# Eight weight buffers instead of six, paid for with slots and work tiles, in a hybrid decoder trunk

## The chip, the core and the metric

The program runs on one core of a Trainium2 chip. The core has five engines that run side by side, each through its own list of instructions in order: TensorE (PE in the profile, its weight loads are PEld), VectorE (DVE), ScalarE (ACT), GpSimd (POOL) and SyncE (SP), which here only issues DMAs. The metric is the device time of one execution in microseconds (us); of several runs the median counts. Both kernels run one program once, with all weights in HBM at the start.

## The reference

The reference is a decoder trunk of two layers on 256 rows of width 1024, all in fp32. Each layer is

```python
h = h + 0.5 * swiglu(rmsnorm(h, ffn1_norm[i]), ffn1_w_gate[i], ffn1_w_up[i], ffn1_w_down[i])
h = h + mixer(rmsnorm(h, mix_norm[i]))        # layer 0: differential attention, layer 1: Mamba-2 SSD
h = h + memory_cross_attention(rmsnorm(h, xa_norm[i]), mem, ...)
h = h + 0.5 * swiglu(rmsnorm(h, ffn2_norm[i]), ffn2_w_gate[i], ffn2_w_up[i], ffn2_w_down[i])

def swiglu(h, w_gate, w_up, w_down):
    return (jax.nn.silu(h @ w_gate) * (h @ w_up)) @ w_down
```

with a last norm behind layer 1. The hidden width of each of the four feed-forward parts (called FFN 1 to 4 below, in order of time) is 2816, so each reads three matrices of 1024 x 2816 numbers. Differential attention subtracts a second softmax, weighted with a scalar lambda made of four small vectors: exp(sum lq1 lk1) - exp(sum lq2 lk2) + 0.2.

## The kernel before

**Weights.** A weight matrix is read in pieces of 1 MB: a tile of 128 x 2048 fp32 numbers out of the pool `wp`, which has 6 buffers. Each piece is worked off in two *grans* of 128 x 1024 (`Gran.split`, lines 207 to 226). For each gran ACT writes `whi`, the piece rounded to fp32r (L224), and DVE writes `wlo`, the rest (L225). TensorE then multiplies three times (`mm3`, L262 to L264): high by high, high by low, low by high. `whi` and `wlo` have 4 buffers each (`hp`), and the grans are split two ahead of the one that TensorE works on (`AHEAD`). A weight buffer comes free when the second gran's `wlo` has been written; only then may SP issue the load that takes its place. SP's queue is in order.

**The sets.** The gate and up projections of an FFN are cut into blocks of 512 columns, c = 0 to 4, and a half block, c = 5. Two of them (in FFN 2 to 4: c = 0 and c = 5) are done plainly. The blocks c = 1 to 4 (in FFN 1: 2 to 4) are each one *set*, made by `seven` in the manner of Strassen: seven products of half the size in each direction instead of eight. With the four weight pieces b11 and b21 (up, first and second half of the rows) and b12 and b22 (gate), the seven right-hand sides are, in the order in which a set uses them: x1 = b11 + b12, then b11, x2 = x1 + b22, b22, x3 = b12 + b22, b21, x4 = x2 + b21. The sums x1 and x2 are DVE additions of a whole piece (L203; x1 takes a buffer of its own, x2 is written over it). x3 and x4 are accumulating DMAs: GpSimd issues two of 512 KB (L199) that read the weight once more and add it onto the buffer, as soon as its earlier content has been split. So a set of 512 columns loads four pieces and two again. Each right-hand side is two grans of six matmuls on TensorE.

**The hosts.** A set has more work for DVE per matmul than a plain product. So `share` mixes other grans, the *hosts*, between the seven products: `counts` gives, for each of the seven positions, how many hosts come before that product. A host is a gran with 12 matmuls. In FFN 2 to 4 the 22 hosts are, in this order, four grans of up of c = 0, four of the half block, and fourteen of the down projection of the hidden blocks that are done (`d0`, `d1`). What the counts don't use comes behind the last set.

**The order.** The kernel is written as a list of units. Every stage calls `pipe.pe(us)` after its matmuls, which advances a written clock; `pipe.after(us, f)` puts a piece of evacuation work f at a due time on that clock. The result is a program order. For the first two units the order of PE, DVE, ACT and SP is kept as written, for the SSD mixer that of PE; for all other units the framework's scheduler orders each engine's instructions by its own estimate of when they can run, with program order as the priority. Each engine's list is fixed when the program is built.

**Other pools.** `slot` hands out 128 x 512 tiles (2 KB on each partition) of the pool `sp`, 32 of them, for everything that lives some time: hidden activations, q, k, v, SSD states. `work` hands out tiles for passing results: up to 256 columns from tag "v" with 9 buffers (1 KB each), else from tag "w" with 10 (2 KB each).

**Lambda.** `lam_col` runs as an extra in the third set of FFN 1. DVE multiplies and sums (L717, L718), ACT takes the exponential (L719), then DVE subtracts (L720) and subtracts 0.2 (L721). The value is read by the softmax of the differential attention (`probs`, L982 on).

Of the kernel before, what the change touches and what calls it, by code (L numbers as in the profile page):

```python
# [12 lines left out]
ALU = mybir.AluOpType  # L13
AX = mybir.AxisListType

P = 128
# [41 lines left out]
def trunk(ctx, tc, a, out):  # L58
    nc = tc.nc


    const = ctx.enter_context(tc.tile_pool(name="const", bufs=1))
    wp = ctx.enter_context(tc.tile_pool(name="wp", bufs=6))
    hp = ctx.enter_context(tc.tile_pool(name="hp", bufs=4))
    xp = ctx.enter_context(tc.tile_pool(name="xp", bufs=8))
    sp = ctx.enter_context(tc.tile_pool(name="sp", bufs=32))
    wk = ctx.enter_context(tc.tile_pool(name="wk", bufs=10))
    sm = ctx.enter_context(tc.tile_pool(name="sm", bufs=3))
    pacc = ctx.enter_context(tc.tile_pool(name="pacc", bufs=8, space=bass.MemoryType.PSUM))
    dram = ctx.enter_context(tc.tile_pool(name="dram", bufs=1, space=bass.MemoryType.DRAM))  # L70
# [9 lines left out]

    def work(name, n=512, dt=F32):

        return wk.tile([P, n], dt, name=name, tag="v", bufs=9) if n <= 256 else wk.tile([P, n], dt, name=name, tag="w")


    ident = const.tile([P, P], F32, name="ident")
# [53 lines left out]
    pipe = Pipe()  # L140
# [171 lines left out]
    def wide(parts, norm, name, fin, eng=None, single=False):  # L312


        ws = [[W(src, k, 4, c0, n) for k in range(0, KT, 4)] for src, c0, n in parts]

        def run(*gr):
            ps = [acc(name) for _ in range(2)]
            for g in use(gr):
                for k in range(g.nk):  # L320
                    kt = g.k0 + k
                    xh, xl = pipe.need(norm.x, kt)
                    if single and kt < 4:

                        for i, (l, r) in enumerate(((xh, g.hi), (xl, g.hi), (xh, g.lo))):
                            for t in range(2):
                                nc.tensor.matmul(ps[t], lhsT=l[:, t * P:(t + 1) * P], rhs=r[:, k, :],
                                                 start=kt == 0 and i == 0, stop=False)
                        pipe.pe(1.36)
                        continue  # L330
                    for t in range(2):
                        ts = slice(t * P, (t + 1) * P)
                        mm3(ps[t], xh[:, ts], xl[:, ts], g.hi[:, k, :], g.lo[:, k, :], kt == 0, kt == KT - 1)
                        pipe.pe(0.68)
            fin(ps)
        cut = [(k, 1) for k in range(KT)] if single else ((0, 2), (2, 2), (4, 2), (6, 2))
        units.append(([Gran(k, nk, *((w[k // 4], 0, n) for w, (_, _, n) in zip(ws, parts)),
                            eng=eng if k in ((3, 5) if single else (6,)) else None) for k, nk in cut], run))

    def stream(parts, norm, name, fin):  # L340

        ws = [Pair(parts, k) for k in range(0, KT, 4)]
        ps = []

        def step(g):
            if not ps:
                ps.extend(acc(name) for _ in range(2))
            for k in range(g.nk):
                kt = g.k0 + k
                xh, xl = pipe.need(norm.x, kt)  # L350
                for t in range(2):
                    ts = slice(t * P, (t + 1) * P)
                    mm3(ps[t], xh[:, ts], xl[:, ts], g.hi[:, k, :], g.lo[:, k, :], kt == 0, kt == KT - 1)
                    pipe.pe(0.68)
            if kt == KT - 1:
                fin(ps)
        return [(Gran(k, 2, (ws[k // 4], 0, 512)), step) for k in (0, 2, 4, 6)]
# [111 lines left out]
    def combine(y, out, waits, pre=()):  # L469

        raw = {}

        def part(t, h):
            return [v2(y[2 * h + p])[:, :, t * P:(t + 1) * P] for p in range(2)]

        def mix(i, l, r, op):
            raw[i] = work("sraw")
            o, l, r = ([v2(x[:, p * S:(p + 1) * S]) for p in range(2)] if not isinstance(x, list) else x
                       for x in (raw[i], raw[l] if isinstance(l, int) else l, r))
            for p in range(2):  # L480
                nc.vector.tensor_tensor(o[p], l[p], r[p], op=op)

        def cut(i):
            hi, lo = slot("s_hi", F32R), slot("s_lo", F32R)
            nc.scalar.copy(hi, raw[i])
            nc.vector.tensor_tensor(lo, raw[i], hi.bitcast(F32), op=ALU.subtract)
            out[i] = (hi, lo)
        steps = [*pre, lambda: mix(0, part(1, 0), part(1, 1), ALU.subtract), lambda: cut(0),
                 lambda: mix(2, 0, part(0, 0), ALU.subtract), lambda: mix(1, 2, part(0, 1), ALU.add), lambda: cut(1),
                 lambda: cut(2), lambda: mix(3, part(0, 0), part(1, 0), ALU.subtract), lambda: cut(3)]  # L490
        for f, w in zip(steps, waits):
            pipe.after(w, f)

    class Norm:
# [15 lines left out]
        def square(self, c):  # L510
            for t in range(2):
                junk = work("sq")
                nc.scalar.activation(junk, h[t][c], AF.Square, accum_out=self.ss[:, 2 * c + t:2 * c + t + 1])
            self.n += 1
            if self.n == 2:
                s = sm.tile([P, 16], F32, name="nsum", tag="nsum")
                nc.vector.tensor_tensor(s[:, 0:2], self.ss[:, 0:2], self.ss[:, 2:4], op=ALU.add)
                self.col = rpow(s[:, 0:2], 1.0 / D, 2, "rcol")
                if self.first:
                    pipe.after(1.5, self.scaled)  # L520
# [134 lines left out]
    lam = const.tile([P, 4], F32, name="lam")  # L655
# [58 lines left out]
    def lam_col():  # L714
        pr = work("lampr", 128).rearrange("p (c d) -> p c d", c=2)
        l4 = lqk.rearrange("p (c t) d -> p c t d", t=2)
        tc.keep_in_program_order(nc.vector.tensor_tensor(pr, l4[:, :, 0, :], l4[:, :, 1, :], op=ALU.mult))  # L717
        nc.vector.tensor_reduce(lam[:, 0:2], pr, axis=AX.X, op=ALU.add)  # L718
        nc.scalar.activation(lam[:, 0:2], lam[:, 0:2], AF.Exp)  # L719
        nc.vector.tensor_tensor(lam[:, 2:3], lam[:, 1:2], lam[:, 0:1], op=ALU.subtract)  # L720
        nc.vector.tensor_scalar(lam[:, 3:4], lam[:, 2:3], 0.2, None, op0=ALU.subtract)  # L721

    nlam = lam[:, 3:4]

# [50 lines left out]
    def ffn_hidden(nm, l, norm, fin, extra=None):  # L775
# [11 lines left out]
        def gate_fin(c):  # L787
            def fin(ps):
                if c == 0:
                    pipe.after(T["gate"], gated(c, ps, 512))  # L790
                else:
                    gated(c, ps, 512)()
            return fin

        def up_fin(c, o=0, n=512):
            def fin(ps):
                if o:
                    gated(c, ps, n)()
                us = box.pop(c)
                for t in range(2):  # L800
                    nc.vector.scalar_tensor_tensor(us[t][:, :n], ps[t][:, o:o + n], norm.col[:, t:t + 1], us[t][:, :n],
                                                   op0=ALU.mult, op1=ALU.mult)
                pipe.after(T["hid"], lambda: turn(c, us, n))
                extras(c)
            return fin
# [53 lines left out]
        wide([(wg, 0, 512)], norm, "gate", gate_fin(0), **({} if units else dict(single=True, eng=nc.gpsimd)))  # L859
        c = HID // 512  # L860
        half = stream([(wg, c * 512, 256), (wu, c * 512, 256)], norm, "gateup", up_fin(c, 256, 256))
        six, eight, ten = [1, 1, 1, 0, 1, 1, 1], [2, 1, 1, 1, 1, 1, 1], [2, 1, 2, 1, 2, 1, 1]
        if norm is first_norm:
            wide([(wu, 0, 512)], norm, "up", up_fin(0))
            n = half + stream([(wg, 512, 512)], norm, "gate", gate_fin(1)) + stream([(wu, 512, 512)], norm, "up", up_fin(1))
            counts = {2: eight, 3: eight, 4: ten}
        else:
            n = stream([(wu, 0, 512)], norm, "up", up_fin(0)) + half
            counts = {1: six, 2: six, 3: six, 4: [1, 0, 1, 0, 1, 0, 1]}
        wd = a[nm + "_w_down"][l]  # L870

        def part(half, ps):
# [9 lines left out]
        for c, k in counts.items():  # L882
            s = seven((wu, c * 512), (wg, c * 512), norm.x, norm.s, seven_fin(c), (0, 1, 3, 2, 5, 4, 6), "dve")
            steps += share(n[:sum(k)], s, k)
            n = n[sum(k):]
# [4 lines left out]
    def ffn(nm, l, norm, nxt, extra=None):  # L890
        fin = upd(0.5, nxt)
        hid, wd = ffn_hidden(nm, l, norm, fin, extra)
        weave(down(wd, 1, [(12, 4), (16, 4)], hid, [], 12, fin))
# [630 lines left out]
    def last(norm):  # L1524
# [48 lines left out]
        def first_half(half, banks):  # L1573
            for t in range(2):
                for q in range(2):
                    evac(banks[t][:, q * 256:(q + 1) * 256], t, q)
        hid, wd = ffn_hidden("ffn2", 1, norm, first_half, {12: final_gain})
        banks = {}

# [91 lines left out]
```

## Time and profile before

| | |
|---|---|
| median of 3 runs | 1277.52 us (1272.74, 1277.52, 1277.61) |
| profiled execution, its own time | 1276.76 us |
| its span, first to last instruction | 1274.9 us |
| mean granted TensorE clock | 0.998 |
| busy share of the span | PE 98%, PEld 84%, DVE 83%, ACT 69%, POOL 13% |
| read from HBM | 267.52 MB |

Outside the span lie 1276.76 - 1274.9 = 1.9 us. A matmul is counted busy from its start to a modelled end, and neighbours overlap; so PE's idle time shows only pauses, and what a pause costs is read from the distance of two starts. Idle time of DVE, ACT and the DMA queues costs nothing in itself; it matters where TensorE waits behind it.

### The profile page before, as it was taken

How to read it: one execution, taken by the hardware profiler on the slowest of the kernel's cores; microseconds unless marked ns; L12 is line 12 of the kernel's file. 1: busy time of each engine (PE TensorE's matmuls, PEld its weight loads, DVE VectorE, ACT ScalarE, POOL GpSimd, SP SyncE). 2: the span in 40 equal slices, each digit the busy share in tenths (PEclk: the TensorE clock that was granted, in tenths of full speed). 3: DMA queues.
4: the chain of work that ended last, by engine and by line, in shares of the span. 5: the costliest groups of instructions: out<-in, count | busy, mean ns of one | idle time of the engine just before them, and what ended most of it. 6: DMA issues, size and time to landing. Idle time of an engine off the chain costs nothing.

```text
span 1274.9 us, 18150 instructions
## 1 busy us (share of the span) xinstructions
PE 1254.1 (98%) x6751; PEld 1070.9 (84%) x6751; DVE 1057.5 (83%) x1451; ACT 877.6 (69%) x1394; POOL 161.4 (13%) x139
## 2 busy tenths in 40 slices
PE   9999999999999999999999999999999999999997
PEld 7778888788988887888887889999998898888786
DVE  6989776886877898888888976798998987998796
ACT  6766765686666876677776766677776775877673
POOL 1111002200100010100101100022222100101110
PEclk9999999999999999999999999999999999999999
DMA  9877965344685688995798986665544685698891
GB/s 334 220 224 237 321 231 168 131 138 161 144 272 150 194 247 248 251 319 157 231 248 237 261 279 193 207 199 166 184 147 165 153 244 166 169 260 220 275 279 36
DMA packets 158315, 269.79 MB, mean 212 GB/s; under 512 B 6889, under 2 KB 43410, under 8 KB 158226
## 3 DMA queue, kind: packets, MB, share of 16 engines
q1 hardware_dynamic: 137744, 229.75, 53.0%
q0 software_dynamic: 19744, 38.28, 17.5%
q8 instruction: 53, 0.87, 0.3%
q10 hardware_dynamic: 738, 0.59, 0.1%
q14 instruction: 36, 0.29, 0.1%
HBM read 267.52 MB, written 1.08 MB: 211 GB/s over the span
## 4 chain that ended last, share of the span: by engine, by line
PE 78%; DVE 9%; DMA 8%; issue 3%; ACT 2%; POOL 0%; POOLq 0%; DVEq 0%; ACTq 0%; SPq 0%
PE out L263 7%; PE out L264 7%; PE out L262 7%; DMA w<-in_ffn_w_gate_dram 7%; PE seven L263 6%; PE seven L264 6%; PE seven L262 6%; DVE wlo L225 4%; PE xs L264 2%; PE xs L262 1%; PE xs L263 1%; DVE w L203 1%; PE mk L262 1%; PE mk L264 1%; PE mk L263 1%
## 5 line engine op out<-in xcount | busy, mean ns | idle before, releaser
L225 DVE TENSOR_TENSOR wlo<-w,whi 128x1024 fp32r<-128x1024 f32 (+2 forms) x532 | 641.4, 1220 | 128.0 <-ACT whi L224 119.5
L224 ACT CAST whi<-w 128x1024 fp32r<-128x1024 f32 (+2 forms) x534 | 551.8, 1040 | 272.8 <-PE out L264 98.3
L262 PE MATMUL out<-whi,hid_hi 128*128 128x512 f32 x336 | 132.5, 394 | 0.0
L263 PE MATMUL out<-wlo,hid_hi 128*128 128x512 f32 x336 | 131.3, 391 | 0.7 <-DVE wlo L225 0.6
L264 PE MATMUL out<-whi,hid_lo 128*128 128x512 f32 x336 | 131.4, 391 | 0.0
L262 PE MATMUL seven<-whi,s_hi 128*128 128x512 f32 x272 | 106.8, 393 | 0.0
L263 PE MATMUL seven<-wlo,s_hi 128*128 128x512 f32 x272 | 106.1, 390 | 0.4 <-DVE wlo L225 0.4
L264 PE MATMUL seven<-whi,s_lo 128*128 128x512 f32 x272 | 106.0, 390 | 0.0
L203 DVE TENSOR_TENSOR w<-w 128x2048 f32<-128x2048 f32 x32 | 73.2, 2288 | 25.7 <-DMA w<-in_ffn_w_gate_dram 24.6
L199 POOL DMA_DIRECT2D w<-in_ffn_w_gate_dram x30 | 36.9, 1467 | 346.3 <-DVE w L203 189.9
L263 PE MATMUL seven<-wlo,xh 128*128 128x512 f32 x180 | 71.0, 394 | 7.5 <-DVE wlo L225 7.4
L263 PEld LDWEIGHTS out<-wlo,hid_hi 128*128 128x128 f32 x336 | 63.2, 188 | 14.9 <-DVE wlo L225 2.3
L264 PEld LDWEIGHTS out<-whi,hid_lo 128*128 128x128 f32 x336 | 63.1, 188 | 14.0 <-DVE hid_lo L855 1.0
L262 PEld LDWEIGHTS out<-whi,hid_hi 128*128 128x128 f32 x336 | 63.1, 188 | 12.4
L262 PE MATMUL seven<-whi,xh 128*128 128x512 f32 x180 | 70.1, 390 | 0.0
L264 PE MATMUL seven<-whi,xl 128*128 128x512 f32 x180 | 70.1, 390 | 0.0
L199 POOL DMA_DIRECT2D w<-in_ffn_w_up_dram x30 | 36.6, 1251 | 233.7 <-DVE wlo L225 221.2
L263 PEld LDWEIGHTS seven<-wlo,s_hi 128*128 128x128 f32 x272 | 51.1, 188 | 10.8 <-DVE wlo L225 0.8
L264 PEld LDWEIGHTS seven<-whi,s_lo 128*128 128x128 f32 x272 | 51.1, 188 | 10.7
L262 PEld LDWEIGHTS seven<-whi,s_hi 128*128 128x128 f32 x272 | 51.1, 188 | 10.0
L263 PEld LDWEIGHTS seven<-wlo,xh 128*128 128x128 f32 x180 | 33.8, 188 | 17.7 <-DVE wlo L225 10.9
L262 PEld LDWEIGHTS seven<-whi,xh 128*128 128x128 f32 x180 | 33.9, 188 | 7.2
(397 smaller groups left out, 3020.9 us busy)
## 6 DMA issues: line engine op xcount, KB each, us to landing
w<-in_ffn_w_up_dram SPq DMA_DIRECT2D x40, 1024.0 KB, 6.8
w<-in_ffn_w_down_dram SPq DMA_DIRECT2D x40, 1024.0 KB, 8.4
w<-in_ffn_w_gate_dram SPq DMA_DIRECT2D x38, 1024.0 KB, 7.9
w<-in_ssd_w_in_dram SPq DMA_DIRECT2D x24, 1024.0 KB, 5.4
w<-in_xa_w_kv_dram SPq DMA_DIRECT2D x16, 1024.0 KB, 5.1
w<-in_ffn_w_gate_dram POOLq DMA_DIRECT2D x30, 512.0 KB, 8.5
w<-in_ffn_w_up_dram POOLq DMA_DIRECT2D x30, 512.0 KB, 7.4
w<-in_da_w_in_dram SPq DMA_DIRECT2D x12, 1024.0 KB, 5.2
```

The lines of the kernel that those rows point to most:

```text
L199: nc.gpsimd.dma_start(self.t[:, k:k + 2, :], w.src[r0:r0 + 2 * P, w.c0:w.c0 + w.n] .rearrange("(k p) c -> p k c", p=P), accum_op=ALU.add)
L203: nc.vector.tensor_tensor(self.t, self.l.t, w.t, op=ALU.add)
L224: nc.scalar.copy(hv, src)
L225: self.eng.tensor_tensor(self.lo[:, :, o:o + n], src, hv.bitcast(F32), op=ALU.subtract)
L262: nc.tensor.matmul(o, lhsT=lh, rhs=rh, start=start, stop=False, skip_group_check=onto)
L263: nc.tensor.matmul(o, lhsT=lh, rhs=rl, start=False, stop=False, skip_group_check=onto)
L264: nc.tensor.matmul(o, lhsT=ll, rhs=rh, start=False, stop=stop, skip_group_check=onto)
```

## The change

The pool `wp` gets 8 buffers instead of 6 (16 KB more on each partition). `sp` falls from 32 to 28 slots (8 KB less), the "w" work tiles from 10 to 7 (6 KB less), the "v" tiles from 9 to 6 (3 KB less). The last two steps of lambda are put at a due time 6.0 us later on the written clock. In FFN 2 to 4 the hosts of the four sets change from 6, 6, 6, 4 to 6, 5, 6, 5: the second set loses the host before its second product (b11), the last set gains one before its sixth product (b21). The order of the 22 hosts stays.

```diff
-    wp = ctx.enter_context(tc.tile_pool(name="wp", bufs=6))
+    wp = ctx.enter_context(tc.tile_pool(name="wp", bufs=8))
...
-    sp = ctx.enter_context(tc.tile_pool(name="sp", bufs=32))
-    wk = ctx.enter_context(tc.tile_pool(name="wk", bufs=10))
+    sp = ctx.enter_context(tc.tile_pool(name="sp", bufs=28))
+    wk = ctx.enter_context(tc.tile_pool(name="wk", bufs=7))
...
-        return wk.tile([P, n], dt, name=name, tag="v", bufs=9) if n <= 256 else wk.tile([P, n], dt, name=name, tag="w")
+        return wk.tile([P, n], dt, name=name, tag="v", bufs=6) if n <= 256 else wk.tile([P, n], dt, name=name, tag="w")
...
         nc.scalar.activation(lam[:, 0:2], lam[:, 0:2], AF.Exp)
-        nc.vector.tensor_tensor(lam[:, 2:3], lam[:, 1:2], lam[:, 0:1], op=ALU.subtract)
-        nc.vector.tensor_scalar(lam[:, 3:4], lam[:, 2:3], 0.2, None, op0=ALU.subtract)
+
+        def minus():
+            nc.vector.tensor_tensor(lam[:, 2:3], lam[:, 1:2], lam[:, 0:1], op=ALU.subtract)
+            nc.vector.tensor_scalar(lam[:, 3:4], lam[:, 2:3], 0.2, None, op0=ALU.subtract)
+        pipe.after(6.0, minus)
...
-        six, eight, ten = [1, 1, 1, 0, 1, 1, 1], [2, 1, 1, 1, 1, 1, 1], [2, 1, 2, 1, 2, 1, 1]
+        five, six = [1, 0, 1, 0, 1, 1, 1], [1, 1, 1, 0, 1, 1, 1]
+        eight, ten = [2, 1, 1, 1, 1, 1, 1], [2, 1, 2, 1, 2, 1, 1]
...
-            counts = {1: six, 2: six, 3: six, 4: [1, 0, 1, 0, 1, 0, 1]}
+            counts = {1: six, 2: five, 3: six, 4: five}
```

## The prediction

> **What bounds the kernel now.** The page first: TensorE is busy for all but 20.8 of 1274.9 us, so the change can win only pauses of TensorE. Next who it waited for, longest in total first:
>
> ```profile
> span 1274.9 us, 18150 instructions
> PE 1254.1 (98%) x6751; PEld 1070.9 (84%) x6751; DVE 1057.5 (83%) x1451; ACT 877.6 (69%) x1394; POOL 161.4 (13%) x139
> ...
> PE seven L263 <- DVE wlo L225: 7.8, 8, 1.9
> PE up L263 <- DVE lam L721: 1.9, 1, 1.9
> ...
> PE xs L264 <- DVE xq_lo L1052: 1.2, 1, 1.2
> PE xs L262 <- ACT xq_hi L1051: 0.7, 1, 0.7
> PE out L263 <- DVE wlo L225: 0.6, 2, 0.3
> ```
>
> The reader sees a dozen short waits, nearly all for DVE's `wlo`. Who held DVE up stands in the waits of DVE, and whom the loads wait for in those of SP's queue:
>
> ```profile
> DVE w L203 <- DMA w<-in_ffn_w_gate_dram: 24.6, 11, 4.5
> SPq L161 <- DVE wlo L225: 791.6, 161, 14.9
> ```
>
> DVE stood 24.6 us before the sums x1 and x2 (L203) until a gate piece had landed; every `wlo` queued behind such a sum stood with it. SP stood 791.6 us until a `wlo` gave a buffer free. So the loop is: buffer free, load, sum, `wlo`, matmul. The chain of waits shows the load in it each time (start, us):
>
> ```profile
> 74.48 9.36 DMA w<-in_ffn_w_gate_dram
> 341.72 12.34 DMA w<-in_xa_w_q_dram
> ...
> 673.57 9.53 DMA w<-in_ffn_w_gate_dram
> ```
>
> One turn of it, in the third set of FFN 4, from the timeline of SP, DVE and PE:
>
> ```profile
> 1163.39 1.22 DVE L225 TENSOR_TENSOR wlo<-w,whi 128x1024 fp32r<-128x1024 f32 x1
> 1166.38 0.37 SPq L161 DMA_DIRECT2D w<-in_ffn_w_down_dram  x1
> 1171.88 0.37 SPq L161 DMA_DIRECT2D w<-in_ffn_w_gate_dram  x1
> 1176.50 1.21 DVE L225 TENSOR_TENSOR wlo<-w,whi 128x1024 fp32r<-128x1024 f32 x1
> 1182.23 2.29 DVE L203 TENSOR_TENSOR w<-w 128x2048 f32<-128x2048 f32 x1 [4.51 <-DMA w<-in_ffn_w_gate_dram]
> 1184.44 1.22 DVE L225 TENSOR_TENSOR wlo<-w,whi 128x1024 fp32r<-128x1024 f32 x1
> 1185.71 0.50 PE L263 MATMUL seven<-wlo,xh 128*128 128x512 f32 x1 [1.90 <-DVE wlo L225]
> 1188.05 0.50 PE L263 MATMUL seven<-wlo,xh 128*128 128x512 f32 x1 [0.67 <-DVE wlo L225]
> ```
>
> SP issues b22 at 1171.88, the moment a buffer comes free; it lands some 10.3 us later, DVE had been free since 1177.71, and TensorE pays 1.90 + 0.67 us.
>
> **The change, part by part.**
>
> *Two more weight buffers.* With eight, each load may start at the buffer release two places earlier in the row. For the b22 above the releases were, going back, 1171.88, 1166.38 (the down load went out on it) and the end of the `wlo` at 1164.61 (1163.39 + 1.22). Issued there, with the same 10.3 us, it lands at about 1174.9, 2.8 us before DVE gets to x2. The 4.51 us go, and both pauses with them. What is late next is the `wlo` queue itself: the second product's `wlo` would be done 4.5 us earlier for a pause of 1.9, so about 2.6 us of slack is left there. The same count for the other loads of the chain moves each of them forward by more than its wait. I take all of these pauses as gone. Two pauses stay, in the first set of FFN 1:
>
> ```profile
> 37.76 0.50 PE L263 MATMUL seven<-wlo,s_hi 128*128 128x512 f32 x1 [0.40 <-DVE wlo L225]
> 47.51 0.50 PE L263 MATMUL seven<-wlo,xh 128*128 128x512 f32 x1 [1.91 <-DVE wlo L225]
> ```
>
> DVE is busy without a break there (it builds the first mixed inputs), and no DMA is late. So of the 7.8 us, 7.8 - 0.40 - 1.91 = 5.5 go, and the 0.6 of `out`. The 1.2 + 0.7 of `xs` in the first cross attention go as well: there ACT's in-order queue stood for a piece of the q weights, with the `xq_hi` that TensorE wanted behind it:
>
> ```profile
> 354.15 1.05 ACT L224 CAST whi<-w 128x1024 fp32r<-128x1024 f32 x1 [2.01 <-DMA w<-in_xa_w_q_dram]
> ```
>
> *The pause called `lam`.* The waits put 1.9 us down to L721, but DVE's rows show the x2 sum before it, held by b22 (issued at 74.48):
>
> ```profile
> 83.93 2.29 DVE L203 TENSOR_TENSOR w<-w 128x2048 f32<-128x2048 f32 x1 [3.27 <-DMA w<-in_ffn_w_gate_dram]
> 86.14 0.15 DVE L720 TENSOR_TENSOR lam<-lam 128x1 f32<-128x1 f32 x1
> 87.34 0.14 DVE L721 TENSOR_SCALAR lam<-lam 128x1 f32<-128x1 f32 x1
> 84.97 0.39 PE L264 MATMUL seven<-whi,s_lo 128*128 128x512 f32 x1
> 85.19 0.39 PE L262 MATMUL up<-whi,xh 128*128 128x512 f32 x1
> 87.48 0.50 PE L263 MATMUL up<-wlo,xh 128*128 128x512 f32 x1 [1.90 <-DVE lam L721]
> 88.00:91.60 3.60, 3.60 (x10) 2.78 (x10) 3.60 (x5) 0.00 (x0) 0.00 (x0) 0.53 0.00 0
> ```
>
> The last row is a stretch (length, busy time and count on PE, PEld, DVE, ACT and POOL, granted clock, DMA share, GB/s). After the pause the clock falls to 0.53: 10 matmuls in 3.60 us, where 16 would start at a distance of 0.22 to 0.23 (84.97 to 85.19). Six missing are 1.4 us. So this place costs 1.9 + 1.4 = 3.3 us, and the earlier load takes it away. Moving L720 and L721 issues the same two instructions later, no DMA, past no queue but DVE's own; it takes 0.15 + 0.14 us out of a stretch that DVE then gets through anyway, and puts them into a later one. I take 0 for it, bounded by 0.3 either way. Without the move DVE, no longer held by x2, could have come to L720 before ACT's exponential was done; the later due time covers that.
>
> The Trainium skill, "TensorE: Matmul & The Clock Gate", section "Part 1: The HAM clock gate (the "warmup" mystery)", says the clock is halved after at least one idle window of about 3.4 us. By that rule a pause of 1.9 us costs itself alone, and the gain of this place would be 1.9 instead of 3.3; the row with 0.53 speaks against it here.
>
> *A pause costs more than the idle time shown.* 85.19 to 87.48 is 2.29 us between two starts that else lie 0.23 apart: 2.06 lost for 1.90 idle. 0.16 more on each of the eleven pauses that go (6 seven, 2 out, 1 up, 2 xs): 1.8 us.
>
> *Slots and work tiles.* These cost where fewer buffers than live tiles are left. I counted, from first write to last read of each tile in the timeline. Of the 405 slot tiles at most 26 live at once (the 26th is written in the first row); of the 181 "w" tiles at most 5; of the 81 "v" tiles at most 6, for under 0.1 us:
>
> ```profile
> 339.87 0.68 DVE L1052 TENSOR_TENSOR xq_lo<-xq,xq_hi 128x512 fp32r<-128x512 f32 x1
> 280.16 0.69 DVE L1025 TENSOR_TENSOR on<-po,orc 128x512 f32<-128x512 f32 x1 [1.12 <-POOL orc L466]
> 960.08 0.40 ACT L1470 ACTIVATE junk<-y 128x256 f32<-128x256 f32 x1
> ```
>
> 28, 7 and 6 are enough. If the buffers go round in order of release, the tightest reuse lies 6.3 us after the release for slots, 8.3 for "w" and 2.2 for "v". Cost 0. Without that cover a waiting `junk` or `yo` would stand at the head of ACT's or DVE's queue with the `whi` and `wlo` behind it; the shortest reach is in the SSD part, eight groups, and I bound it by 0 to 0.4 us (one `junk`) for each.
>
> *The hosts.* The last set has the front x1, b11, host, x2 after the change as before; its new host comes behind x3, before b21, and gives 12 x 0.23 = 2.7 us of matmuls before x4 is wanted. Before, x4 was late there:
>
> ```profile
> 1239.55 1.05 ACT L224 CAST whi<-w 128x1024 fp32r<-128x1024 f32 x1 [1.24 <-DMA w<-in_ffn_w_up_dram]
> 533.27 0.50 PE L263 MATMUL seven<-wlo,xh 128*128 128x512 f32 x1 [0.43 <-DVE wlo L225]
> 1207.40 2.29 DVE L203 TENSOR_TENSOR w<-w 128x2048 f32<-128x2048 f32 x1 [1.56 <-DMA w<-in_ffn_w_gate_dram]
> ```
>
> That wait didn't reach TensorE, so the host gains cover and no time. The second set takes over the short front: TensorE comes to b11 and x2 2.7 us earlier, DVE only one `wlo` (1.2 us) earlier. The nearest rows are the last set's, which had that front: up to 0.7 us of pauses in a set (the 0.43 above and one `out` of the waits, 0.6 / 2), and that with x1 held up by its load (1.56 us above). In the second set x1 waited 1 us or less. So 0 to 0.7 for each of three sets; I take 0.3: 0.9 us.
>
> **Sum**, against the profiled execution (1276.76 us, 0.76 under the median of the runs): 5.5 + 0.6 + 1.9 + 3.3 + 1.8 = 13.1 gained, 0.9 lost: 1264.6, against the median 1265.3. I say **1265 us**. Bounds: everything gone, the first set's 2.3 us too, gives about 1261; slots and hosts at their worst (8 x 0.4 + 3 x 0.7 = 5.3 in place of 0.9) about 1270.
>
> **The rivals.**
>
> *DVE stays behind* (chance 0.20). Each engine's list is ordered anew by the scheduler's estimate; if x1 and x2 are put earlier because their loads come earlier, DVE may meet another late piece, and the `wlo` behind it wait as before. For: DVE is 83% busy on the whole. Against: 24.6 us of its waits are for these loads alone. About half of the gain stays: 1271 (1268 to 1274).
>
> *The buffers bring no earlier load* (0.12): the change doesn't do what it says. SP's queue is in order, so a load that is due early can stand behind one that still waits. For: the rows tell only that the load in front waited for its buffer, not what the one behind it would do. Against: the releases two places back were there each time. Then 1276 to 1278.
>
> *Slower: x4's accumulating DMAs come too late* (0.10). Two more megabytes may be under way when they are issued.
>
> ```profile
> 1190.62 2.44 POOL L199 DMA_DIRECT2D w<-in_ffn_w_up_dram  x2 [17.99 <-DVE wlo L225]
> 1205.92 1.05 ACT L224 CAST whi<-w 128x1024 fp32r<-128x1024 f32 x1 [0.45 <-PE out L264]
> w<-in_ffn_w_up_dram POOLq DMA_DIRECT2D x30, 512.0 KB, 7.4
> w<-in_xa_w_kv_dram SPq DMA_DIRECT2D x16, 1024.0 KB, 5.1
> ```
>
> In the third set of FFN 4 they are issued from 1190.62 on, and the `whi` of x4 starts at 1205.92, 15.3 us later. 1.2 + 7.4 us leaves about 6.7; behind two more loads of 5.1 us it would be 3.5 too late, which the split's lead of two grans covers only in part. Over 15 sets it decides from 0.9 us a set (13.1 / 15); at 1.5 it gives 22.5 - 13.1 = +9.4: 1287. Against: the loads start earlier and so end earlier, and their number is the same; ACT waited for x4 only 1.24 us even in the last set.
>
> The Trainium skill, "DMA: Bandwidth & Descriptors", section "Queues, rings and completion order", says that each DMA engine takes turns between the queues that have work, packet by packet. By that rule more loads waiting on SP's queue take no larger share from GpSimd's than one does, and this rival falls away; no row here shows the turns.
>
> **How the numbers follow.** Forecast 0.58, with 1260 to 1269; the rivals 0.20, 0.12 and 0.10. The range of 8 in 10 takes in the forecast, the first rival and most of the second: 1260 to 1277. A measurement of this kernel tells about 0.5% from no change, 6.4 us. Faster by more (under 1271.1): all of the forecast and half of the first rival, 0.67; within 0.5%: the rest of that one, the second and a part of the third, 0.25; slower 0.08.
>
> **What would show it.** Right: in DVE's waits, L203 for the gate pieces falls from 24.6 to under 5 us; PE's waits for `wlo` in `seven` from 7.8 to about 2.5, all in FFN 1; no stretch with the clock at 0.5 near 88 us; no `xs` wait in the first cross attention; ACT's wait for x4 gone. Wrong: DVE still standing at L203; new waits for slots, named by `slot` or `work` tiles; `whi` of x4 waiting for in_ffn_w_up; pauses at b11 or x2 of the second set above 0.7 us.

## The result, and the profile after

| | before | after |
|---|---|---|
| median | 1274.70 us (1272.55 to 1278.11, 7 runs) | 1269.06 us (1267.77 to 1270.46, 7 runs) |
| ratio, 95% interval | | 0.9948 [0.9932, 0.9965] |
| the same two kernels on a second chip | 1271.78 us (29 runs) | 1270.74 us (12 runs), 0.999 [0.9976, 1.0005] |
| profiled execution: own time, span | 1276.76, 1274.9 us | 1269.06, 1267.2 us |

The kernel became faster by 5.6 us in the first measurement. In the second the medians differ by 1.0 us, and the interval takes in no change at all. Neither is the 12.2 us forecast. One of the 29 runs, of 1778.78 us at a mean clock of 0.655, was a slow one and is not in the ratios. The profiled executions differ by 7.7 us of span. The page of the kernel after:

```profile
span 1267.2 us, 18142 instructions
...
PE 1251.8 (99%) x6751; PEld 1070.5 (84%) x6751; DVE 1057.7 (83%) x1451; ACT 878.6 (69%) x1394; POOL 161.6 (13%) x139
```

TensorE is idle for 15.4 us now, 5.4 less than before. Whom it waited for (total, times, longest):

```profile
PE seven L263 <- DVE wlo L225: 2.2, 2, 1.9
PE seven L262 <- DVE p L830: 1.8, 3, 0.9
...
PE gate L327 <- ACT whi L224: 1.0, 1, 1.0
PE gate L263 <- DVE wlo L225: 1.0, 2, 0.8
PE out L264 <- DVE hid_lo L858: 0.9, 1, 0.9
```

Of the pauses that the prediction quoted only the two in the first set of FFN 1 are left, but three names are new: `p`, `gate` (in FFN 1, at 7, 14 and 68 us) and `hid_lo`. What held DVE up and what held SP up:

```profile
DVE w L203 <- DMA w<-in_ffn_w_gate_dram: 6.2, 6, 2.3
```

```profile
SPq L161 <- DVE wlo L225: 781.5, 159, 15.1
```

DVE's wait before the sums fell from 24.6 to 6.2 us. SP waits for buffers about as long as before (791.6): it doesn't wait less, it waits for releases that lie earlier. The turn of the loop that the prediction followed, b22 of the third set of FFN 4, now looks like this (SP, then DVE):

```profile
1155.10 0.37 SPq L161 DMA_DIRECT2D w<-in_ffn_w_gate_dram  x1
```

```profile
1169.01 1.21 DVE L225 TENSOR_TENSOR wlo<-w,whi 128x1024 fp32r<-128x1024 f32 x1
1170.15 2.28 DVE L203 TENSOR_TENSOR w<-w 128x2048 f32<-128x2048 f32 x1
1172.35 1.22 DVE L225 TENSOR_TENSOR wlo<-w,whi 128x1024 fp32r<-128x1024 f32 x1
```

The load goes out 15.1 us before its sum, and the row of the sum has no bracket any more: DVE doesn't stand there.

Where the 7.7 us of span came from, from the first matmul of one part to that of the next in the traces (us; the kernel with the pools alone, `e1_pools`, is the first experiment):

| | before | after | pools alone |
|---|---|---|---|
| to the first product of FFN 1's first set | 37.0 | 37.7 | 37.8 |
| rest of FFN 1 | 158.31 | 157.05 | 156.80 |
| differential attention | 136.49 | 136.48 | 136.48 |
| first cross attention | 80.98 | 78.47 | 78.49 |
| FFN 2 | 178.56 | 177.93 | 175.60 |
| FFN 3 | 190.79 | 189.50 | 188.59 |
| SSD mixer | 227.78 | 227.65 | 227.66 |
| second cross attention | 79.63 | 79.61 | 79.61 |
| FFN 4 | 178.96 | 176.37 | 175.20 |
| from the last matmul's end to the end of the span | 6.42 | 6.41 | 6.43 |

The last two columns hold the main finding. Between these executions the pools alone took 12.2 us off the span; the rest of the change gave 4.5 of them back, nearly all in FFN 2 to 4 (2.33, 0.91 and 1.17). These are single executions. That of the kernel before lies 2 to 5 us above its medians, so the medians put the gain of the pools lower, at 7.7 to 8.3 us (below). A second execution with the pools alone (`e15_pools_again`) took 0.8 us more in FFN 2 and 1.0 more in FFN 3, so the 0.91 of FFN 3 says nothing; FFN 4 differs by 0.02.

### The profile page after: what moved, and what is told of

It is laid out like the page before. It is cut to its first block, busy times and chain, and to the rows that moved or that the text cites. A ratio compares the mean times of both kernels' runs of the same rounds, so it can differ in the third digit from the quotient of the medians.

```text
span 1267.2 us, 18142 instructions
## 1 busy us (share of the span) xinstructions
PE 1251.8 (99%) x6751; PEld 1070.5 (84%) x6751; DVE 1057.7 (83%) x1451; ACT 878.6 (69%) x1394; POOL 161.6 (13%) x139
## 4 chain that ended last, share of the span: by engine, by line
PE 87%; DVE 7%; issue 2%; DMA 2%; ACT 2%; POOL 0%; POOLq 0%; DVEq 0%; ACTq 0%
PE out L264 9%; PE out L263 8%; PE out L262 8%; PE seven L262 8%; PE seven L263 7%; PE seven L264 7%; DVE wlo L225 3%; PE xs L264 2%; DMA w<-in_ffn_w_gate_dram 2%; PE xs L262 2%; PE xs L263 2%; PE mk L262 1%; PE xq L263 1%; PE mk L264 1%; PE xq L264 1%
## 5 line engine op out<-in xcount | busy, mean ns | idle before, releaser
L203 DVE TENSOR_TENSOR w<-w 128x2048 f32<-128x2048 f32 x32 | 73.2, 2286 | 6.3 <-DMA w<-in_ffn_w_gate_dram 6.2
L264 PEld LDWEIGHTS seven<-whi,xl 128*128 128x128 f32 x180 | 33.9, 189 | 7.1
```

The source lines that it names most:

```text
L203: nc.vector.tensor_tensor(self.t, self.l.t, w.t, op=ALU.add)
L264: nc.tensor.matmul(o, lhsT=ll, rhs=rh, start=False, stop=stop, skip_group_check=onto)
```

## The experiments

Twelve kernels in three groups of four, each group on one chip beside fresh runs of the kernel before: its medians there were 1272.75 (23 runs), 1271.78 (29 runs) and 1272.74 us (14 runs). The theory at the start: the buffers carry the gain, the hosts and lambda move little. The rivals: the scheduler's new order of DVE's list takes a part back; or the hosts do.

### The parts by themselves

`e1_pools`: only the four buffer numbers of the change.

```diff
-            counts = {1: six, 2: five, 3: six, 4: five}
+            counts = {1: six, 2: six, 3: six, 4: [1, 0, 1, 0, 1, 0, 1]}
...
-        pipe.after(6.0, minus)
+        minus()
```

(the diff is against the kernel after). Expected:

> The kernel before with the pools of the change alone (wp 8, sp 28, wk 7 and 6), lambda and the hosts as before. Theory A (the earlier loads bring the whole gain, the new hosts of the second set cost 2.3 us: three pauses of 0.46 + 0.88 + 0.46 us idle before x3, for DVE's subtraction p at the line of c12, with 0.16 more on each): ratio to before 0.994 (7.9 us faster), no PE wait of seven for p, the pauses of the sets 3 and 4 in FFN 2 to 4 gone. Theory B (the hosts carry a part of the gain, the pools less): ratio 0.997 or above, pauses in the last sets left.

Measured: 1264.48 us (1263.64 to 1266.62, 6 runs), ratio 0.9937 [0.9925, 0.995]. TensorE's waits:

```profile
PE gate L263 <- DVE wlo L225: 2.6, 1, 2.6
PE seven L263 <- DVE wlo L225: 2.1, 2, 1.9
```

Apart from the start two pauses in FFN 1 are left; no `p`, no `hid_lo`, and in FFN 2 to 4 one pause of 0.2 us (three, the longest 0.5, in `e15_pools_again`). So the pools are the whole gain, 8.3 us on this chip, and more than the change brings there (`e7_lam_undone` below: 2.8). DVE's wait is another matter:

```profile
DVE w L203 <- DMA w<-in_ffn_w_gate_dram: 14.6, 10, 3.2
```

The faster kernel has more than twice the 6.2 us of the kernel after, and 16.6 in `e15_pools_again`. This sum doesn't tell how late TensorE is: it counts where TensorE runs out of `wlo` behind it, and in FFN 2 to 4 it hardly does here.

`e2_hosts_undone`: the kernel after with the old hosts, that is pools and lambda.

```diff
-            counts = {1: six, 2: five, 3: six, 4: five}
+            counts = {1: six, 2: six, 3: six, 4: [1, 0, 1, 0, 1, 0, 1]}
```

> The changed kernel with the hosts of before (6, 6, 6, 4). Theory A: 2 us faster than the changed kernel, ratio 0.994 to 0.993, no PE wait of seven for p; the last sets stay without pauses, since x1 is no longer late there. Theory B: slower than the changed kernel, ratio 0.996 or above, with pauses for wlo back in the last sets.

Measured: 1265.72 us (1263.99 to 1271.03), 0.995 [0.9932, 0.9968]; no wait for `p`. Its profiled execution was a long one (span 1269.2), with a pause of 1.5 us in FFN 3 behind an early sum. Within the intervals it is the same as the pools alone.

`e3_hosts_alone`: the kernel before with the new hosts.

```diff
-            counts = {1: six, 2: six, 3: six, 4: [1, 0, 1, 0, 1, 0, 1]}
+            counts = {1: six, 2: [1, 0, 1, 0, 1, 1, 1], 3: six, 4: [1, 0, 1, 0, 1, 1, 1]}
```

> The kernel before with the new hosts alone. Theory A: 2 us slower than before, ratio 1.001 to 1.002: the second set pauses for p, and the pauses of the last set (0.43, 0.35 and 0.27 idle) stay, because its front is the same. Theory B: faster than before, ratio 0.998 or less.

Measured: 1277.36 us (1273.55 to 1285.91, 12 runs), 1.0045 [1.0028, 1.0063]: 4.6 us slower than before, where 2 were expected. No wait for `p` here; with six buffers the pauses come elsewhere, three for a `wlo` of the down projection in the last sets (TensorE's waits):

```profile
PE out L263 <- DVE wlo L225: 5.1, 3, 2.2
PE seven L263 <- DVE wlo L225: 4.5, 6, 1.9
```

The longest, in FFN 4 (timeline, DVE, then PE): DVE stands 1.81 us at a `hid_lo` for ACT's `hid_hi`, and the `wlo` that TensorE wants is behind it.

```profile
1220.04 1.29 DVE L855 TENSOR_TENSOR hid_lo<-htp,hid_hi 128x512 fp32r<-128x512 f32 x2 [1.81 <-ACT hid_hi L854]
1221.24 2.35 DVE L225 TENSOR_TENSOR wlo<-w,whi 128x1024 fp32r<-128x1024 f32 x2
```

```profile
1222.51 0.80 PE L263 MATMUL out<-wlo,hid_hi 128*128 128x512 f32 x1 [2.25 <-DVE wlo L225]
```

`e7_lam_undone`: the kernel after with lambda's end at its old place.

```diff
-        pipe.after(6.0, minus)
+        minus()
```

> The changed kernel with the end of lambda at its old place. Theory A: no difference to the changed kernel within 0.3 us, ratio 0.9948. Rival: with x2 no longer late, DVE comes to the first subtraction before ACT's exponential is done, waits for it 1 us or more and holds the wlo behind it: a PE pause near 80 us, 1 to 2 us slower than the changed kernel, ratio 0.996.

Measured: 1269.95 us (1268.14 to 1273.91, 12 runs), 0.9978 [0.9963, 0.9993]. It has the same waits as the kernel after: `p` 1.4 us in three, `hid_lo` 1.0, and none for `lam`. Against `e1_pools` on the same chip it differs by the hosts alone: 1269.95 - 1264.48 = 5.5 us. Lambda's move shows no effect that the runs can tell, here or in `e2_hosts_undone` (1.2 us above `e1_pools`, inside the intervals).

### Which order of DVE costs

The kernel after showed DVE's x1 sums (L203) far ahead in its list. In FFN 2 the x1 sum of the third set (timeline, DVE, then PE):

```profile
473.50 2.28 DVE L203 TENSOR_TENSOR w<-w 128x2048 f32<-128x2048 f32 x1
475.70 0.68 DVE L858 TENSOR_TENSOR hid_lo<-htp,hid_hi 128x512 fp32r<-128x512 f32 x1
476.31 2.35 DVE L225 TENSOR_TENSOR wlo<-w,whi 128x1024 fp32r<-128x1024 f32 x2
478.57 0.68 DVE L830 TENSOR_TENSOR p<-p,seven 128x512 f32<-128x512 f32 x1
```

```profile
479.31 0.50 PE L262 MATMUL seven<-whi,s_hi 128*128 128x512 f32 x1 [0.46 <-DVE p L830]
```

The sum stands 22 us ahead of its product (495.3) and in front of the `p` of the second set, whose PSUM bank the x3 product needs. With the pools alone `p` comes first:

```profile
479.17 0.68 DVE L827 TENSOR_TENSOR p<-p,seven 128x512 f32<-128x512 f32 x1
...
481.88 2.29 DVE L203 TENSOR_TENSOR w<-w 128x2048 f32<-128x2048 f32 x1 [0.79 <-DMA w<-in_ffn_w_gate_dram]
```

At the end of FFN 2 of the kernel after the same happens with the first sum of FFN 3, ahead of both `hid_lo`, and there its load isn't even landed:

```profile
568.88 2.29 DVE L203 TENSOR_TENSOR w<-w 128x2048 f32<-128x2048 f32 x1 [0.83 <-DMA w<-in_ffn_w_gate_dram]
571.08 0.68 DVE L858 TENSOR_TENSOR hid_lo<-htp,hid_hi 128x512 fp32r<-128x512 f32 x1
```

```profile
571.82 0.73 PE L264 MATMUL out<-whi,hid_lo 128*128 128x512 f32 x2 [0.88 <-DVE hid_lo L858]
```

`e5_after_again`: the kernel after, unchanged, as the mark of the second chip.

> The changed kernel once more, as the mark for the three others and for what differs from one execution to the next. Expected 0.995 to before, pauses at the same places as in the first profile, but the 3.4 us at half clock, which stood behind the pause at 48 us in the first profile and behind the one at 85 us in the kernel before, at another place or missing: whether a pause is followed by it is chance, so it is no term of any edit.

Measured: 1270.74 us (1268.13 to 1275.43, 12 runs), 0.999 [0.9976, 1.0005], not the 0.995 expected. The same list, another execution (DVE, then PE):

```profile
573.11 2.29 DVE L203 TENSOR_TENSOR w<-w 128x2048 f32<-128x2048 f32 x1 [2.53 <-DMA w<-in_ffn_w_gate_dram]
```

```profile
576.05 0.50 PE L264 MATMUL out<-whi,hid_lo 128*128 128x512 f32 x1 [2.59 <-DVE hid_lo L858]
```

The place that cost 0.88 us before costs 2.59 here, because the load lands 1.7 us later, counted from the FFN's first matmul. A sum put ahead of a load that hasn't landed makes the time hang on that load. At 68 us, in FFN 1, the pause is 2.58 in place of 0.81.

`e8_front_kept`: the kernel after, the second set gives up the host before b21 and keeps the one before b11.

```diff
-            counts = {1: six, 2: five, 3: six, 4: five}
+            counts = {1: six, 2: [1, 1, 1, 0, 1, 0, 1], 3: six, 4: five}
```

> The changed kernel, with the second set's host taken away before b21 (1, 1, 1, 0, 1, 0, 1) and its front left as before. Theory L (the lost host in the front makes DVE late): the three pauses of seven for p go, 2.3 us faster than the changed kernel. Theory S (the scheduler puts the DVE sum x1 of the next set earlier, ahead of what TensorE wants, since its loads come earlier): the pauses for p may go or move, but pauses behind early sums stay, gain under 1.5 us.

Measured: 1270.06 us (1268.02 to 1273.58), 0.9987 [0.9977, 0.9997]. The three `p` waits are gone and nothing is won. The wait for `hid_lo` stays (3.25 us in its profile), and in FFN 4, which has no pause of 0.3 us or more, the kernel needs 176.36 us against 175.20 with the pools alone: seven distances between starts of 0.33 to 0.45 us instead of 0.23, in four places, 69 to 107 us after the FFN's first matmul. So what the hosts cost is not the `p` waits alone: the seven distances add up to 1.0 of the 1.16 us.

`e10_sums_in_order`: the kernel after, the sums kept in program order on DVE.

```diff
-                nc.vector.tensor_tensor(self.t, self.l.t, w.t, op=ALU.add)
+                tc.keep_in_program_order(nc.vector.tensor_tensor(self.t, self.l.t, w.t, op=ALU.add))
```

> The changed kernel, with each DVE sum x1 and x2 held at its place in program order, so that the scheduler can't move it forward; the loads stay early. Theory S: the pause for gate near 68 us, those for p in the second sets and that for hid_lo near 571 us go, 3 to 5 us faster than the changed kernel (ratio to before 0.991 to 0.9925), and DVE's waits for gate pieces at the sums fall from 6.2 us to under 3. Theory L: the sums now come just before the wlo that need them, the second set's short front still has DVE late, pauses at b11 or x2 of that set; no faster than the changed kernel.

Measured: 1270.13 us (1269.38 to 1273.6, 12 runs), 0.9984 [0.997, 0.9997]. DVE has no wait left for a gate piece, and `p`, `hid_lo` and the pause at 68 us are gone. In their place (TensorE's waits, then one of them in the timeline):

```profile
PE seven L263 <- DVE wlo L225: 6.0, 8, 0.8
PE seven L262 <- ACT whi L224: 1.5, 4, 0.8
```

```profile
470.76 0.50 PE L263 MATMUL seven<-wlo,s_hi 128*128 128x512 f32 x1 [0.76 <-DVE wlo L225]
```

That is x2 of the second set; the last set has the same, in each of FFN 2, 3 and 4. The last set pauses 0.25 us more just before it, which it doesn't with the old hosts (next run). With the sums late, the short front pays at x2; with the sums early, at `p`.

`e11_pools_sums_in_order`: the same line on the pools alone.

> The kernel before with the pools of the change alone and the sums held in program order. Theory S: the pause of 2.65 us for gate near 68 us goes, 2 to 3 us faster than the pools alone, ratio 0.991 to 0.992, DVE's waits at the sums fall from 14.6 to under 5 us. Rival: sums late make wlo late, pauses at x2; no faster than the pools alone (0.9937).

Measured: 1264.82 us (1264.7 to 1266.73, 5 runs), 0.9945 [0.9932, 0.9959]. It has the pause of 0.77 only in the last sets, the only ones with the short front here. `e10` and `e11` differ by the hosts and lambda: 5.3 us. FFN 1 gains most, 154.75 us from the first set on against 156.80 with the sums free; FFN 2 to 4 lose it again (2.9 us against `e1`, 1.1 against `e15`), so the whole is no faster.

### What is left, and how many buffers

`e15_pools_again`, the mark of the third group:

> The change of the pools alone once more, as the mark for the other three on the same chip: 1263.6 to 1266.6 us, ratio 0.9937 within 0.002. If the ratio lies above 0.996 here, the gain of the pools is no steadier than that of the whole change.

Measured: 1265.01 us (1263.93 to 1266.15, 6 runs), 0.9938 [0.9923, 0.9953]. The gain of the pools repeats, 7.7 us here against 8.3; that the ratios agree to 0.0001 is chance, their intervals are 0.0013 to 0.0015 to either side.

`e13_pools_second_five`: the pools alone, the second set with the change's five hosts, the last set as before; the host left over comes behind the last set.

```diff
-            counts = {1: six, 2: six, 3: six, 4: [1, 0, 1, 0, 1, 0, 1]}
+            counts = {1: six, 2: [1, 0, 1, 0, 1, 1, 1], 3: six, 4: [1, 0, 1, 0, 1, 0, 1]}
...
-        assert not n
-        weave(steps + d0[7:])
+        weave(steps + n + d0[7:])
```

> The change of the pools alone, with one host taken from the second set (before b11, as in the change) but not given to the last set: it comes behind the last set. Theory: the second set's short front is what the new hosts cost; then FFN 2, 3 and 4 are each 0.6 to 1.5 us longer than with the pools alone, TensorE waits for p or for wlo at the second set's front, and the time is 1266.5 to 1269. Rival: the host that the last set gains is what costs (it reorders the end of the FFN); then the time is that of the pools alone within 1 us, about 1264.5, and no pause for p is seen.

Measured: 1268.12 us (1266.96 to 1269.18, 9 runs), 0.9963 [0.9951, 0.9975]. The early sum and the `p` wait are back, with the last set untouched (DVE's timeline, then TensorE's waits):

```profile
473.08 2.28 DVE L203 TENSOR_TENSOR w<-w 128x2048 f32<-128x2048 f32 x1
...
478.15 0.68 DVE L827 TENSOR_TENSOR p<-p,seven 128x512 f32<-128x512 f32 x1
```

```profile
PE seven L262 <- DVE p L827: 1.4, 3, 0.5
```

So the second set's short front costs 1268.12 - 1265.01 = 3.1 us of the 5.5. About 2.4 are left for the last set's new host, by subtraction across two groups of runs on one chip; no run had that host alone. The traces show where it costs: at the end of FFN 2. In all four executions with eight buffers, the new host and free sums (the kernel after, `e5`, `e7`, `e8`) the first sum of FFN 3 stands ahead of both `hid_lo`, and TensorE pauses 0.9 to 3.3 us; in the five without the host (`e1`, `e2`, `e12`, `e13`, `e15`) it stands behind them, and there is no pause. In this run:

```profile
565.72 1.29 DVE L855 TENSOR_TENSOR hid_lo<-htp,hid_hi 128x512 fp32r<-128x512 f32 x2 [0.74 <-ACT hid_hi L854]
567.74 2.29 DVE L203 TENSOR_TENSOR w<-w 128x2048 f32<-128x2048 f32 x1 [0.74 <-DMA w<-in_ffn_w_gate_dram]
```

FFN 4 has no such end, and there this run takes as long as the kernel after (176.48 against 176.37): the last set's host costs nothing in it.

`e12_pools_ffn1_in_order`: the pools alone, the sums kept in program order in FFN 1 only.

```diff
-                nc.vector.tensor_tensor(self.t, self.l.t, w.t, op=ALU.add)
+                add = nc.vector.tensor_tensor(self.t, self.l.t, w.t, op=ALU.add)
+                if self.hold:
+                    tc.keep_in_program_order(add)
...
-            s = seven((wu, c * 512), (wg, c * 512), norm.x, norm.s, seven_fin(c), (0, 1, 3, 2, 5, 4, 6), "dve")
+            s = seven((wu, c * 512), (wg, c * 512), norm.x, norm.s, seven_fin(c), (0, 1, 3, 2, 5, 4, 6), "dve", norm is first_norm)
```

(The flag is handed on from `seven` to its two sums.)

> The change of the pools alone, with the hosts and lambda of before, and with the x1 and x2 sums of FFN 1 kept in program order; all other units are ordered freely. Theory: of what the larger pool leaves on the table, the largest piece is the x1 sum that stands in DVE's list ahead of a gate piece that hasn't landed, near 68 us in FFN 1 (TensorE paused 2.65 us there in the kernel with the pools alone, and FFN 1 was 2.0 us shorter with the sums in order). Then this kernel has no pause near 68 us, none in the last sets (0.77 each with all sums in order), and is 2 us below the kernel with the pools alone: about 1262.5 us, ratio near 0.992. Rival: the piece is late whatever the order, and the pause only moves to another instruction: same time as the pools alone, about 1264.5, with a pause of over 1 us elsewhere between 55 and 100 us.

Measured: 1262.28 us (1261.82 to 1264.01, 6 runs), 0.9918 [0.9903, 0.9933], the fastest kernel of the study: 2.7 us under the pools alone. What went is this place (`e15_pools_again`, DVE and PE):

```profile
64.87 2.29 DVE L203 TENSOR_TENSOR w<-w 128x2048 f32<-128x2048 f32 x1 [3.11 <-DMA w<-in_ffn_w_gate_dram]
67.08 2.35 DVE L225 TENSOR_TENSOR wlo<-w,whi 128x1024 fp32r<-128x1024 f32 x2
```

```profile
68.35 0.50 PE L263 MATMUL gate<-wlo,xh 128*128 128x512 f32 x1 [2.52 <-DVE wlo L225]
```

In `e12` DVE does `wlo` and `p` there, and the sum only at 78.61 us:

```profile
63.08 0.68 DVE L829 TENSOR_TENSOR p<-p,seven 128x512 f32<-128x512 f32 x1
63.77 1.22 DVE L227 TENSOR_TENSOR wlo<-w,whi 128x1024 fp32r<-128x1024 f32 x1
66.01 2.59 DVE L227 TENSOR_TENSOR wlo<-w,whi 128x1024 fp32r<-128x1024 f32 x2 [1.01 <-ACT whi L226]
68.52 0.68 DVE L834 TENSOR_TENSOR p<-p,seven 128x512 f32<-128x512 f32 x1
```

FFN 1 took 156.80 us in this execution, no less than the 156.85 of `e15`: a stretch at half clock, some 1.6 us, followed its pause at 48 us, and none came in `e15`. `e11` has the same order in FFN 1, no such stretch, and 154.75 us. So the gain is shown by the medians and by the pause that went, not by the length of FFN 1 in this trace.

`e14_pools_seven`: the pools alone with 7 buffers.

```diff
-    wp = ctx.enter_context(tc.tile_pool(name="wp", bufs=8))
+    wp = ctx.enter_context(tc.tile_pool(name="wp", bufs=7))
```

> The change of the pools alone, with 7 weight buffers instead of 8. Each load may then start one buffer release earlier than before the change instead of two. Theory: most waits of DVE for a gate piece were shorter than the distance of two releases (4.51 us against 1171.88 - 1166.38 = 5.5 us for the longest pause of before), so one more buffer gives nearly all: 1264 to 1267, with DVE's waits at L203 for the gate pieces under 17 us. Rival: each buffer gives its half: 1268 to 1269, and TensorE still pauses for wlo in FFN 2 to 4.

Measured: 1279.65 us (1279.01 to 1281.87, 6 runs), 1.0055 [1.0039, 1.0071]. Both theories missed: this kernel is slower than the one before, with six. The two differ in the slots and work tiles as well. DVE's waits, SP's waits, and from the timeline one of TensorE's ten pauses for `wlo` in FFN 2 to 4 (DVE, then PE):

```profile
DVE w L203 <- DMA w<-in_ffn_w_gate_dram: 28.1, 12, 4.6
```

```profile
SPq L161 <- DVE wlo L225: 850.0, 162, 16.5
```

```profile
526.59 2.29 DVE L203 TENSOR_TENSOR w<-w 128x2048 f32<-128x2048 f32 x1 [3.11 <-DMA w<-in_ffn_w_gate_dram]
528.80 1.22 DVE L225 TENSOR_TENSOR wlo<-w,whi 128x1024 fp32r<-128x1024 f32 x1
```

```profile
530.07 0.50 PE L263 MATMUL seven<-wlo,xh 128*128 128x512 f32 x1 [1.92 <-DVE wlo L225]
```

DVE waits longer for the gate pieces than with six (28.1 against 24.6), and SP longer for its buffers (850.0 against 791.6). Counted from the first matmul of FFN 2 (411.86 here, 412.75 before), the x1 sum of the last set starts 2.3 us earlier than before (529.79), and its piece, issued at 516.70 against 520.03, went out 2.4 us earlier: the wait was only moved in front of a `wlo` that TensorE wanted. Why SP's list with seven buffers waits longer was not tried, and the smaller slot and work pools were not run with six, so how much of the loss is theirs is open.

## Why the prediction was right and wrong

It said 1265 us, by 13.1 gained and 0.9 lost. The first measurement lies 4 us above, the second 6, both within its range of 1260 to 1277. That says little: the range reaches up to the time that the kernel before had when the prediction was made.

**The loop of buffer, load, sum, `wlo`: right in the main.** All pauses of FFN 2 to 4 that it quoted are gone, and with the hosts of before the b22 load of FFN 4's third set goes out at 1157.50 - 1081.0 = 76.5 us after the FFN's first matmul, before it was 1171.88 - 1089.5 = 82.4. That is 5.9 us earlier; the prediction had 7.3. The sign on DVE's wait asked for under 5 us; it is 6.2, and 14.6 to 19.5 with the pools alone (`e1`, `e15`, `e2`), where the scheduler put sums earlier with the loads (the x1 sum of FFN 2's last set 110.2 us after the FFN's first matmul in `e15` and 117.0 before, waiting 2.4 and 2.6 us). In the profiled executions the pools took 12.2 us off the span, against 13.1; in medians 7.7 to 8.3. The sum without the hosts' 0.9 gives 1264.4 us, and `e1_pools` measured 1264.48. A part of that is luck: FFN 1 gave 2 us less than reckoned, and other parts made up for it.

**`xs` in the first cross attention: right.** 1.9 us and two times 0.16 were forecast, 2.5 came in every kernel with the larger pool, 2.2 where all sums were kept in order (`e10`, `e11`).

**FFN 2 to 4: right.** The 6.1 us of pauses and 0.16 more on each of the eight there made 7.4; the pools alone gave 2.96 + 2.20 + 3.76 = 8.9 in `e1`, 7.1 in `e15` and 6.4 in `e2`, each against the one profiled execution of before.

**The place called `lam`: half wrong.** The pause at 87 us went, as forecast. But FFN 1 gained only 1.3 us from its first set on, 1.5 with the pools alone, where 3.5 was in the sum. "DVE meets another late piece", the first rival, came true in FFN 1. The x1 sum moved from 69.84 to 65.16 us, ahead of its load (before, then after):

```profile
69.84 2.29 DVE L203 TENSOR_TENSOR w<-w 128x2048 f32<-128x2048 f32 x1 [1.79 <-DMA w<-in_ffn_w_gate_dram]
65.16 2.29 DVE L203 TENSOR_TENSOR w<-w 128x2048 f32<-128x2048 f32 x1 [1.41 <-DMA w<-in_ffn_w_gate_dram]
```

TensorE paused at 68 us for 0.81 us (0.84 in `e13`, 2.4 to 3.1 in six other executions with eight buffers and free sums). `e12` shows the price against `e15`: 2.7 us. With the sums in order and no half clock FFN 1 takes 154.75 us (`e11`), and the sum had 158.31 - 3.5 = 154.8.

The other fault is the 1.4 us for the half clock, booked on one edit though it belongs to an execution. The stretch at 88 us is gone and a new one follows the pause at 48, which was there before without it (length, busy time and count on PE, PEld, DVE, ACT and POOL, then the clock, 0.56):

```profile
48.30:51.70 3.40, 3.40 (x9) 2.71 (x10) 3.26 (x3) 1.57 (x3) 0.98 (x1) 0.56 0.69 203
```

The new stretch explains the short pause at 68 us. Only the two executions with it (the kernel after, `e13`) pause 0.8 us there; TensorE comes some 1.6 us later to the same late piece, and FFN 1 takes 157.05 us in both. In `e1`, `e7` and `e15`, without it, the pause is 2.4 to 2.6 us and FFN 1 takes 156.80 to 157.10. So the half clock cost the kernel after nearly nothing there, and the late piece alone made FFN 1 fall short.

**The hosts: the step that failed.** The prediction put 0.9 us on the second set's short front (bounds 0 to 2.1 for the three sets) and nothing on the last set. It cost 3.1 for the second set, and 4.6 to 5.5 for both in three pairs (`e3` against before, `e7` against `e1`, `e10` against `e11`). The working looked at who is late when DVE's order stays as it is: b11 and x2. In that order (`e10`) x2 of the second set does pause, 0.76 us in each of the three FFNs where 0.3 was taken from 0 to 0.7, and the last set is not free. With the sums left to the scheduler, fewer hosts move its estimate, and with it the sums of the next set, in front of `p` and `hid_lo`; the working left that out. Either order costs about the same, 5.3 and 5.5 us, so the moved sums are where the cost shows, and not the whole reason for it: the term was mis-sized in both. What the prediction took for a rival of the buffers, a sum put ahead of its late piece, is in the kernels with the old hosts a matter of FFN 1 above all; in FFN 2 and 3 TensorE pays 0.2 to 0.5 us for it at a place (1.5 once, in `e2`).

**Slots, work tiles, x4, lambda: right at nothing.** TensorE, DVE and ACT have no wait that the traces put down to a slot or a work tile, and the SSD mixer, where the prediction saw the shortest reach, takes 227.65 us against 227.78. What the smaller pools do to the scheduler's order is not separated from the buffers: no run had the one without the other. ACT waits for a piece of the up projection only once, 2.7 us at 24.6 us, before the first set; its wait for x4 in the last set of FFN 4 (1.24 us) is gone. So the third rival, x4 too late, didn't come: two more loads under way kept no accumulating DMA back. Lambda's move shows nothing in `e2` against `e1` and in `e7` against the kernel after.

**The baseline.** The sum was made against an execution of 1276.76 us. The kernel before has medians of 1271.78 to 1274.70 in all later runs, and the highest of them counts the three runs known before the prediction. So by the medians some 2 to 5 us of the 13.1 belonged to that execution and not to the kernel, and the ratio missed by more than the time did: 12.2 / 1277 = 0.96% forecast, 0.52% and 0.1% measured.

## What to carry to other kernels

Where a scheduler orders the engines' lists, a buffer count or a host is also an edit of that order: look after each for sums that now stand in front of loads not landed, or in front of work that frees a PSUM bank. More buffers aren't monotone: six, seven and eight gave 1272.7, 1279.7 and 1265.0 us on one chip (six with the larger slot and work pools). And measure a bundle's parts by themselves: here one part carried 8 us and another gave 5 back; without it, and with one list kept in order, the kernel reached 1262.28.

## What the runs showed of the chip

The half clock is not fixed to a pause. The pause of 1.9 us at 47 to 49 us stands in 13 of the 14 profiled executions (all but `e10`), as in the row below; a stretch of starts 0.43 us apart, 3.4 us long, followed it in 3 of the 13 (the kernel after, `e12`, `e13`). Going by the granted clock, 10 of the 14 executions have such a stretch behind this or another pause; `e1`, `e7`, `e11` and `e15` have none.

```profile
47.72 0.50 PE L263 MATMUL seven<-wlo,xh 128*128 128x512 f32 x1 [1.89 <-DVE wlo L225]
```

```profile
48.30:51.70 3.40, 3.40 (x16) 2.77 (x15) 3.17 (x4) 2.24 (x4) 1.46 (x2) 1.00 0.83 266
```

Those are rows of `e1`, from the timeline and, last, a stretch of it: the same pause, then a clock of 1.00 and 16 matmuls where the kernel after has 9. It also followed pauses as short as 0.77 and 0.83 us (`e10`, at 39 to 41 us). The Trainium skill, "TensorE: Matmul & The Clock Gate", section "Part 1: The HAM clock gate (the "warmup" mystery)", asks for an idle window of about 3.4 us before the clock falls; no pause here was that long, and the clock fell behind some of them. The whole runs follow the clock as well: the kernel before took 1275.5 us at a mean clock of 0.996 and 1270.7 at 0.999 on one chip (medians of 2 and 4 runs), so a difference of 5 us between single runs can be chance.
